# Attention in a two-layer step: full-height low-part score passes, and both heads' products with the values in alternation

## The chip, the cores and the metric

The kernel runs on one core of a Trainium2 chip. The metric is device time in microseconds for one execution. On the core, TensorE (PE in the profile) multiplies matrices, with its weight loads listed apart as PEld; VectorE (DVE), ScalarE (ACT) and GpSimd (POOL) do the elementwise work; SyncE (SP) issues nearly all DMA transfers. Each engine works through its own queue in order; the order of instructions in each queue is fixed when the kernel is built.

## The reference, cut to what matters

One inference step of a two-layer backbone over 128 prompt tokens and 256 sample tokens, width 1024. Layer 0 mixes tokens by attention, layer 1 by a gated MLP; each is followed by a gated feed-forward block. The change lies in layer 0's attention, 16 heads of 64 features:

```
# prompt: each head, 128 queries against 128 keys
s = einsum('bhqd,bhkd->bhqk', q, k) * HEAD_DIM ** -0.5
o = einsum('bhqk,bhkd->bhqd', softmax(s), v)

# sample: 256 queries on a grid of 4 rows x 64 columns; a window of all rows and 16 columns
# with a bias per head, and 128 cached context keys, in one softmax
s_win = einsum('bhqd,bhiqjd->bhqij', q_r, k_win) * scale + bias
s_ctx = einsum('bhqd,bhcd->bhqc', q_r, k_ctx) * scale
p = softmax(concatenate([s_win, s_ctx]))
o = einsum('bhqij,bhiqjd->bhqd', p_win, v_win) + einsum('bhqc,bhcd->bhqd', p_ctx, v_ctx)
```

All arithmetic is float32.

## The kernel before, in words

Features lie on partitions, the 384 tokens (prompt first) along the free axis. Every float32 operand of the large products is split exactly into a high and a low part (type fp32r): `load` brings a weight unit into `st` and writes `hi` (ACT) and `lo` (DVE); `mac` makes one product in three passes, high times high, high times low, low times high.

Attention goes over eight pairs of heads (`t`). For a pair, `keys(t)` takes 24 matmuls (8 feature tiles, three passes), copies the keys to `kT` beside the cached ones and splits them into `ks`, one tile per head: the high part on the 64 rows of the head, the low part on the other 64. `queries(t)` takes 24 matmuls and writes, per head, `qd` (the high part, twice over the 128 rows, by ACT) and its rows of `ql` (the low part, by DVE), one tile for both heads in two buffers. So `score` needs two passes: `qd` against all 128 rows of `ks`, then `ql` against the high part of the keys, which are the head's 64 rows only. `bias(t)` brings the position bias by four transfers into `btr` (one buffer) and adds the mask into `bt`.

`scores(t, hh)` makes a head's scores: two query blocks of the sample over 384 columns, one block of the prompt over 128, two passes each, so six matmuls, in two PSUM banks (`ps_sc`). DVE adds the bias and takes maxima, ACT does the exponential, DVE scales; the results are `pr` and `pc`. `values(t, ps)` turns the probabilities head by head: seven transposes (bank `ta`, then `tb`), two ACT copies into `pT`, and then that head's four products with the values, plain float32, each recorded as two matmul instructions of 64 columns. Head 0 takes columns 0 to 63 of the array, head 1 columns 64 to 127; results of both go to one bank `pv`, which is split into `ohi` and `olo` for the output projection.

Inside a pair the program order is scores of head 0, keys of the next pair, its bias, scores of head 1, queries of the next pair, values of the pair before, and then three units of the modulations (`ada.load(3)`, `ada.run(3)`: 24 instructions of 32 columns on the four column groups of the array). The framework takes program order as priority and moves an instruction up or down where operands are late by its own estimate, so that values and modulations stand among the first head's scores in PE's queue. The last pair's values come in the output projection, behind its second output tile.

The instructions in question: L462 and L463 are the two score passes, L524, L528 and L529 the transposes, L525 and L530 the copies to `pT`, L532 and L535 the products with the values, L190 the modulations, L103 to L105 the passes of `mac`.

Of the kernel before, what the change touches and what calls it, by code (L numbers as in the profile page):

```python
# [15 lines left out]
P = 128  # L16
D = 1024
KD = D // P                 # feature tiles of the model width
NPR = 128                   # prompt tokens
NSA = 256                   # sample tokens  # L20
NT = NPR + NSA              # all tokens, prompt first
GROUPS = ((0, 0, NPR), (1, NPR, NT))   # (conditioning, first token, end)
HD = 64
NPAIR = 8
E2 = 2048                   # gMLP width
# [7 lines left out]
# columns of the packed per-feature parameters  # L33
# [6 lines left out]
def backbone(ctx: ExitStack, tc: tile.TileContext, xT_in, cond_in, condr_in, b_ada_in, prm_in,  # L40
# [28 lines left out]
    nc.scalar.activation(zero, zero, AF.Silu)       # loads the table  # L69
# [7 lines left out]
    # TensorE runs at half its clock until it has been busy for a while  # L77
# [23 lines left out]
    def mac(out, a, b, start, stop):  # L101
        """out (+)= a.T @ b, both as (hi, lo)"""
        nc.tensor.matmul(out, a[0], b[0], start=start, stop=False)  # L103
        nc.tensor.matmul(out, a[0], b[1], start=False, stop=False)  # L104
        nc.tensor.matmul(out, a[1], b[0], start=False, stop=stop)  # L105
# [30 lines left out]
    def ada_block(f, tpool=ps_tb):  # L136
        """shift and scale of layer 0's mixer for feature tile f; TensorE's column groups take
        (half of the conditioning, shift or scale)"""
        pa = bank(ps_ad)
        w = ada_load(f) if f else w_first  # L140
        for kk in range(4):
            for hf in range(2):
                for q in range(2):
                    j = 2 * hf + q
                    nc.tensor.matmul(pa[32 * j:32 * j + 32, 0:P], cond_s[:, 4 * hf + kk, :],  # L145
                                     w[hf][:, kk, P * q:P * q + P], start=(kk == 0),
                                     stop=(kk == 3), tile_position=(0, 32 * j))
        sb = tmp.tile([P, 256], F32, name="ada_sb", tag="ada_sb")
        nc.scalar.copy(sb[:, :P], pa[:, :P])
        tp = bank(tpool)  # L150
        nc.tensor.transpose(tp[:, :P], sb[:, :P], ident)
        t = tp[:, :P].rearrange("p (h q r) -> p h q r", h=2, r=32)
        m = mods[0][:, 0:2, f]
        nc.vector.tensor_tensor(m, t[:, 0, :, 0:2],
                                b_ada[:, 0, 0:16].rearrange("p (q k) -> p q k", q=2)[:, :, f]
                                .unsqueeze(2).to_broadcast([P, 2, 2]), ALU.add)
        nc.vector.tensor_tensor(m, m, t[:, 1, :, 0:2], ALU.add)
        gain(0, CM, slice(f, f + 1))

    class Ada:  # L160
        """pieces of 1024 modulations on TensorE, one unit (a feature tile of the conditioning)
        at a time; units are loaded ahead of their products"""
# [35 lines left out]
        def flush(self):  # L198
            """[32j + conditioning, 256 columns] to features on partitions"""
# [18 lines left out]
    class AdaV:  # L218
        """modulations on VectorE, 128 at a time"""
# [40 lines left out]
    sq = {}  # L260

    def square(k, tag="t384"):
        """the last tile's squares are kept apart, to shorten what follows them"""
# [11 lines left out]
    def sums(pin=False):  # L275
        """every token's sum of squares"""
# [9 lines left out]
    def rms(ss=None, pin=False):  # L286
        """1/rms of every token, on all partitions: [P, NT] in PSUM"""
# [12 lines left out]
    def rsqrt(src, v, scale):  # L300
        """(src * scale + EPS) ** -0.5, refined by one Newton step"""
# [11 lines left out]
    # the modulated input of a layer's first products; its last two columns are the shifts  # L313
# [14 lines left out]
    # So that TensorE needn't wait for 1/rms, the first products of a layer take x * gain in place of  # L328
    # h and, in two more columns, the shifts; 1/rms and the shifts' products join them afterwards:
    # W.T @ h = (W.T @ (x * gain)) * R + W.T @ shift  # L330
# [9 lines left out]
    def norm_first(nxt, units):  # L340
        """the first tiles' products as the tiles of x come, then h; returns the banks and R"""
# [13 lines left out]
    def late(ps, R, wkp):  # L355
        """products with 1/rms, and the shifts' products to add to them"""
# [23 lines left out]
    def attention(pool, wkp):  # L380
        # 0 where key column cc is in the window of query column c, else NEG
# [15 lines left out]
        # V, all its tiles at once, as the tiles of h come  # L397
# [25 lines left out]
        # Scores are exact to float32 in two passes: the high part of q stands twice over the 128  # L423
        # rows, against the high and low parts of k; then its low part against the high part of k.
        # Head hh has its high part in rows hs.
# [18 lines left out]
        def queries(t):  # L444
# [5 lines left out]
            ql = wkp.tile([P, NT], F32R, name="ql", tag="ql", bufs=2)  # L450
            for hh in range(2):
# [3 lines left out]
                nc.vector.scalar_tensor_tensor(ql[a], pq[a, :NT], HD ** -0.5,  # L455
# [3 lines left out]
        def score(out, hh, q, ks, qs, cs):  # L459
            qd, ql = q  # L460
            a = HS[hh]
            nc.tensor.matmul(out, qd[hh][:, qs], ks[hh][:, cs], start=True, stop=False)  # L462
            nc.tensor.matmul(out, ql[a, qs], ks[hh][a, cs], start=False, stop=True)  # L463

        def bias(t):
            """relative position bias of query (row rr, column c) to key column cc, slot = key row -
            query row + 3 + rr; rpb_in has its columns reversed, so that both steps are positive"""
# [20 lines left out]
        def scores(t, hh, q, ks, bt):  # L488
            """softmaxes of a head: sample query blocks over window and cache, prompt"""
# [23 lines left out]
        def values(t, ps):  # L513
            """probabilities times values of both heads, as the pair's features"""
            pv = bank(ps_mm)
            for hh in range(2):
                pr, pc = ps[hh]
                hs = slice(64 * hh, 64 * hh + 64)
                pT = wkp.tile([P, 896], F32, name="pT", tag="pT", bufs=2)
                ta = bank(ps_ta)  # L520
                for kb in range(2):
                    for b in range(2):
                        o = kb * 256 + b * P
                        nc.tensor.transpose(ta[:, o:o + P], pr[:, b, kb * P:kb * P + P], ident)  # L524
                nc.scalar.copy(pT[:, 0:512], ta)  # L525
                tb = bank(ps_tb)
                for b in range(2):
                    nc.tensor.transpose(tb[:, b * P:b * P + P], pr[:, b, 256:384], ident)  # L528
                nc.tensor.transpose(tb[:, 256:384], pc, ident)  # L529
                nc.scalar.copy(pT[:, 512:896], tb[:, :384])  # L530
                vs = slice(P * t + 64 * hh, P * t + 64 * hh + 64)
                nc.tensor.matmul(pv[hs, 0:NPR], V[:, 0, vs], pT[:, 768:896], start=True, stop=True,  # L532
                                 tile_position=(0, 64 * hh))
                for i, vv in enumerate((V[:, 1, vs], V[:, 2, vs], cv[:, vs])):
                    nc.tensor.matmul(pv[hs, NPR:NT], vv, pT[:, 256 * i:256 * i + 256],  # L535
                                     start=(i == 0), stop=(i == 2), tile_position=(0, 64 * hh))
            split(ohi[t], olo[t], pv[:, :NT])

        # the values of a pair of heads come one pair after its scores
        kT, qT, bt = keys(0), queries(0), bias(0)  # L540
        old = None
        for t in range(NPAIR):
            new = [scores(t, 0, qT, kT, bt)]
            if t < NPAIR - 1:
                kT2 = keys(t + 1)
                bt2 = bias(t + 1)
            new.append(scores(t, 1, qT, kT, bt))
            if t < NPAIR - 1:
                qT, kT, bt = queries(t + 1), kT2, bt2
            if old is not None:  # L550
                values(t - 1, old)
# [5 lines left out]
        for m in range(KD):  # L557
# [7 lines left out]
            else:  # L565
                residual(0, GM, m, po, (0, SF, CF))
            if m == 1:
                values(NPAIR - 1, old)
# [6 lines left out]
    def conv(l, i, ps, wkp, tag):  # L575
        """ps: the tile's products, in PSUM or in SBUF"""
# [55 lines left out]
    def gmlp(pool, wkp):  # L632
        # a quarter of vn makes room for the low parts of four groups' results
# [95 lines left out]
def _layout(inp):  # L729
# [3 lines left out]
    def feat(a):        # (..., n*128) -> (128, ..., n)  # L733
# [13 lines left out]
    def units(w):       # (K, M) -> (M/128, 128 of K, K/128, 128 of M)  # L747
# [4 lines left out]
    # layer 0's first shifts and scales by feature tile and half of the conditioning  # L752
    w_ada0 = w_ada[0, :, :2 * D].reshape(2, 4, P, 2, KD, P).transpose(4, 0, 2, 1, 3, 5)
    # blocks of 128 modulations over all of the conditioning
# [43 lines left out]
```

## Time and profile before

| | |
|---|---|
| time, median of 3 runs | 1047.04 us (1046.14 to 1047.27) |
| profiled execution, span of the core | 1046.2 us |
| granted TensorE clock, mean | 0.990 |
| PE busy | 1027.7 us, 98% |
| DVE busy | 796.9 us, 76% |
| ACT busy | 496.8 us, 47% |
| mean DMA rate | 167 GB/s |

The page gives the span of the profiled execution, from the first to the last instruction, and no time of its own beside it; the median of the runs lies 0.8 us above that span. A busy time counts every instruction from its start to its end. Matmuls overlap in the array, so for PE the distance between two starts is the cost of the first of them. In the rows, `128*64` after the operands is the shape of the array that a matmul uses (rows, columns); behind it stand the partitions and columns of the data.

### The profile page before, as it was taken

How to read it: one execution, taken by the hardware profiler on the slowest of the kernel's cores; microseconds unless marked ns; L12 is line 12 of the kernel's file. 1: busy time of each engine (PE TensorE's matmuls, PEld its weight loads, DVE VectorE, ACT ScalarE, POOL GpSimd, SP SyncE). 2: the span in 40 equal slices, each digit the busy share in tenths (PEclk: the TensorE clock that was granted, in tenths of full speed). 3: DMA queues.
4: the chain of work that ended last, by engine and by line, in shares of the span. 5: the costliest groups of instructions: out<-in, count | busy, mean ns of one | idle time of the engine just before them, and what ended most of it. 6: DMA issues, size and time to landing. Idle time of an engine off the chain costs nothing.

```text
span 1046.2 us, 16013 instructions
## 1 busy us (share of the span) xinstructions
PE 1027.7 (98%) x5964; PEld 959.3 (92%) x5964; DVE 796.9 (76%) x1697; ACT 496.8 (47%) x862; POOL 13.3 (1%) x27
## 2 busy tenths in 40 slices
PE   7999999999999999999999999999999999999996
PEld 6787777679999999999998889999999999999995
DVE  3557666628899898999989979888599777777653
ACT  3357566536765544433346344444375544453330
POOL 1000000000000000000000000000000000000000
PEclk8999999999999999999999999999999999999998
DMA  7867666515255454566665765665414434435521
GB/s 274 310 191 208 187 186 194 192 61 171 81 153 181 161 156 150 161 199 211 217 196 174 247 205 157 198 191 195 144 65 157 142 122 123 134 109 169 163 69 61
DMA packets 64717, 174.32 MB, mean 167 GB/s; under 512 B 18800, under 2 KB 24064, under 8 KB 64640
## 3 DMA queue, kind: packets, MB, share of 16 engines
q1 hardware_dynamic: 63632, 171.46, 52.1%
q8 instruction: 47, 0.77, 0.3%
q0 software_dynamic: 432, 1.06, 0.3%
q10 hardware_dynamic: 576, 0.79, 0.2%
q14 instruction: 30, 0.25, 0.1%
HBM read 170.66 MB, written 2.62 MB: 166 GB/s over the span
## 4 chain that ended last, share of the span: by engine, by line
PE 92%; DMA 3%; DVE 2%; ACT 1%; SPq 1%; issue 1%; POOL 0%; POOLq 0%; DVEq 0%
PE bank L103 27%; PE bank L105 27%; PE bank L104 27%; DMA btr<-in_rpb 2%; PE bank L535 2%; PE bank L463 1%; PE bank L462 1%; PE bank L687 1%; PE bank L190 1%; PE bank L145 1%; PE bank L524 1%; DMA adw<-in_w_ada 1%; PE bank L532 1%; SPq L471 1%; PE bank L294 1%
## 5 line engine op out<-in xcount | busy, mean ns | idle before, releaser
L96 ACT CAST hi<-st 128x1024 fp32r<-128x1024 f32 (+1 forms) x216 | 222.5, 1032 | 315.3 <-PE bank L104 260.3
L105 PE MATMUL bank<-hhi,lo 128*128 128x384 f32 (+1 forms) x960 | 325.6, 339 | 0.4 <-DVE lo L97 0.4
L103 PE MATMUL bank<-hhi,hi 128*128 128x384 f32 (+1 forms) x960 | 325.7, 339 | 0.0
L104 PE MATMUL bank<-hlo,hi 128*128 128x384 f32 (+1 forms) x960 | 325.1, 339 | 0.0
L97 DVE TENSOR_TENSOR lo<-st,hi 128x1024 fp32r<-128x1024 f32 (+1 forms) x216 | 259.7, 1203 | 80.7 <-ACT hi L96 80.3
L103 PEld LDWEIGHTS bank<-hhi,hi 128*128 128x128 f32 x960 | 181.2, 189 | 3.5 <-issue 3.0
L105 PEld LDWEIGHTS bank<-hhi,lo 128*128 128x128 f32 x960 | 181.2, 189 | 1.3 <-DVE lo L97 0.7
L104 PEld LDWEIGHTS bank<-hlo,hi 128*128 128x128 f32 x960 | 180.6, 188 | 0.1
L248 DVE CUSTOM_DVE_ANT_0 junk<-adw,cs 128x1024 bf16<-128x1024 f32 x112 | 136.7, 1220 | 1.0
L105 PE MATMUL bank<-ahi,lo 128*128 128x384 f32 x352 | 119.0, 338 | 0.0
L104 PE MATMUL bank<-alo,hi 128*128 128x384 f32 x352 | 119.0, 338 | 0.0
L103 PE MATMUL bank<-ahi,hi 128*128 128x384 f32 x352 | 118.8, 338 | 0.0
L105 PEld LDWEIGHTS bank<-ahi,lo 128*128 128x128 f32 x352 | 66.1, 188 | 0.0
L104 PEld LDWEIGHTS bank<-alo,hi 128*128 128x128 f32 x352 | 66.1, 188 | 0.0
L103 PEld LDWEIGHTS bank<-ahi,hi 128*128 128x128 f32 x352 | 66.1, 188 | 0.0
L103 PE MATMUL bank<-hi,hhi 128*128 128x512 f32 x144 | 58.3, 409 | 1.8 <-ACT hhi L322 1.8
L105 PE MATMUL bank<-hi,hlo 128*128 128x512 f32 x144 | 57.5, 399 | 0.0
L104 PE MATMUL bank<-lo,hhi 128*128 128x512 f32 x144 | 57.4, 399 | 0.0
L368 DVE SCALAR_TENSOR_TENSOR x<-bank,mod,x 128x128 f32<-128x128 f32 x64 | 23.9, 413 | 37.6 <-PE bank L105 37.6
L103 PE MATMUL bank<-mhi,hi 128*128 128x384 f32 x128 | 43.4, 339 | 0.0
L105 PE MATMUL bank<-mhi,lo 128*128 128x384 f32 x128 | 43.2, 338 | 0.0
L104 PE MATMUL bank<-mlo,hi 128*128 128x384 f32 x128 | 43.1, 337 | 0.0
(151 smaller groups left out, 1288.7 us busy)
## 6 DMA issues: line engine op xcount, KB each, us to landing
st<-in_w_up SPq DMA_DIRECT2D x88, 512.0 KB, 3.5
adw<-in_w_adaT SPq DMA_DIRECT2D x56, 512.0 KB, 3.6
adw<-in_w_ada SPq DMA_DIRECT2D x40, 512.0 KB, 5.8
st<-in_w_down SPq DMA_DIRECT2D x32, 512.0 KB, 3.6
st<-in_w_qk SPq DMA_DIRECT2D x16, 512.0 KB, 6.7
st<-in_w_gu SPq DMA_DIRECT2D x16, 512.0 KB, 4.2
st<-in_w_gv SPq DMA_DIRECT2D x16, 512.0 KB, 4.3
st<-in_w_gout SPq DMA_DIRECT2D x16, 512.0 KB, 4.2
```

Source lines behind the costliest of these rows:

```text
L96: nc.scalar.copy(hi[:, :n], st[:, :n])
L97: nc.vector.tensor_tensor(lo[:, :n], st[:, :n], hi[:, :n].bitcast(F32), ALU.subtract)
L103: nc.tensor.matmul(out, a[0], b[0], start=start, stop=False)
L104: nc.tensor.matmul(out, a[0], b[1], start=False, stop=False)
L105: nc.tensor.matmul(out, a[1], b[0], start=False, stop=stop)
L145: nc.tensor.matmul(pa[32 * j:32 * j + 32, 0:P], cond_s[:, 4 * hf + kk, :], w[hf][:, kk, P * q:P * q + P], start=(kk == 0), stop=(kk == 3), ...
L190: nc.tensor.matmul(self.pa[32 * j:32 * j + 32, 0:256], cond_s[:, k, :], t[:, 256 * j:256 * j + 256], start=(k == 0), stop=(k == KD - 1), t ...
L248: tc.keep_in_program_order(nc.vector.tensor_tensor_reduce(self.junk, t, self.cs[c], 1.0, 0.0, ALU.mult, ALU.add, m[:, c:c + 1]))
L294: mm = nc.tensor.matmul(R[:, b * P:(b + 1) * P], r[:, b:b + 1].to_broadcast([P, P]), ident, start=True, stop=True)
L368: nc.vector.scalar_tensor_tensor(x[m][:, a:b], ps[:, a:b], mod(l, gate, m, c), x[m][:, a:b], ALU.mult, ALU.add)
L462: nc.tensor.matmul(out, qd[hh][:, qs], ks[hh][:, cs], start=True, stop=False)
L535: nc.tensor.matmul(pv[hs, NPR:NT], vv, pT[:, 256 * i:256 * i + 256], start=(i == 0), stop=(i == 2), tile_position=(0, 64 * hh))
```

## The change

Three things, and comments are dropped throughout.

1. `ql` becomes one tile per head, made once, 128 rows high. The half that doesn't belong to the head is set to zero once by POOL. DVE writes the head's half as before. The second score pass takes all 128 rows of `ql[hh]` against all 128 rows of `ks[hh]`; the zero rows meet the low part of the keys.
2. `values` is cut in two. `turned(hh, ps)` makes the seven transposes and two copies of one head, into `pT` with a tag per head and one buffer each. Head 0 of the pair before is turned after the scores of head 0, head 1 after the keys and the bias of the next pair. In the output projection the last pair is turned behind the first and the second output tile.
3. `values(t, pT)` then makes the products of both heads, head by head in turn for each operand, the sample's first and the prompt's last.

```
+        ql = [pool.tile([P, NT], F32R, name=f"ql{hh}") for hh in range(2)]
+        for hh in range(2):
+            nc.gpsimd.memset(ql[hh][64 * (1 - hh):64 * (1 - hh) + 64].bitcast(F32), 0.0)
...
-            ql = wkp.tile([P, NT], F32R, name="ql", tag="ql", bufs=2)
...
-                nc.vector.scalar_tensor_tensor(ql[a], pq[a, :NT], HD ** -0.5,
+                nc.vector.scalar_tensor_tensor(ql[hh][a], pq[a, :NT], HD ** -0.5,
                                                qd[hh][a].bitcast(F32), ALU.mult, ALU.subtract)
...
-            a = HS[hh]
             nc.tensor.matmul(out, qd[hh][:, qs], ks[hh][:, cs], start=True, stop=False)
-            nc.tensor.matmul(out, ql[a, qs], ks[hh][a, cs], start=False, stop=True)
+            nc.tensor.matmul(out, ql[hh][:, qs], ks[hh][:, cs], start=False, stop=True)
...
+        def turned(hh, ps):
+            pr, pc = ps[hh]
+            pT = wkp.tile([P, 896], F32, name="pT", tag=f"pT{hh}", bufs=1)
+            ta = bank(ps_ta)
+            for kb in range(2):
+                for b in range(2):
+                    o = kb * 256 + b * P
+                    nc.tensor.transpose(ta[:, o:o + P], pr[:, b, kb * P:kb * P + P], ident)
+            nc.scalar.copy(pT[:, 0:512], ta)
+            tb = bank(ps_tb)
+            for b in range(2):
+                nc.tensor.transpose(tb[:, b * P:b * P + P], pr[:, b, 256:384], ident)
+            nc.tensor.transpose(tb[:, 256:384], pc, ident)
+            nc.scalar.copy(pT[:, 512:896], tb[:, :384])
+            return pT
+
+        def values(t, pT):
             pv = bank(ps_mm)
+            def part(hh, cols, vv, o, n, start, stop):
+                nc.tensor.matmul(pv[64 * hh:64 * hh + 64, cols], vv[:, P * t + 64 * hh:P * t + 64 * hh + 64],
+                                 pT[hh][:, o:o + n], start=start, stop=stop, tile_position=(0, 64 * hh))
+
+            for i, vv in enumerate((V[:, 1], V[:, 2], cv)):
+                for hh in range(2):
+                    part(hh, slice(NPR, NT), vv, 256 * i, 256, i == 0, i == 2)
             for hh in range(2):
...
+                part(hh, slice(0, NPR), V[:, 0], 768, 128, True, True)
             split(ohi[t], olo[t], pv[:, :NT])
...
             new = [scores(t, 0, qT, kT, bt)]
+            if old is not None:
+                pT = [turned(0, old)]
             if t < NPAIR - 1:
                 kT2 = keys(t + 1)
                 bt2 = bias(t + 1)
+            if old is not None:
+                pT.append(turned(1, old))
             new.append(scores(t, 1, qT, kT, bt))
             if t < NPAIR - 1:
                 qT, kT, bt = queries(t + 1), kT2, bt2
             if old is not None:
-                values(t - 1, old)
+                values(t - 1, pT)
...
+            if m == 0:
+                pT = [turned(0, old)]
             if m == 1:
-                values(NPAIR - 1, old)
+                pT.append(turned(1, old))
+                values(NPAIR - 1, pT)
```

More of the change, by code (lines that the diff above doesn't have):

```diff
@@ L511, in scores @@
             return pr, pc
-        def values(t, ps):
-            pv = bank(ps_mm)
-            for hh in range(2):
[L517 to L536, printed above, removed]
@@ L541, in attention @@
         old = None
+        pT = None
         for t in range(NPAIR):
             new = [scores(t, 0, qT, kT, bt)]
+            if old is not None:
+                pT = [turned(0, old)]
             if t < NPAIR - 1:
```

## The prediction

> **What bounds the kernel now.** I read the line of the engines on the page first. TensorE (PE) is busy throughout, so a change of PE work can move the end.
>
> ```profile
> span 1046.2 us, 16013 instructions
> PE 1027.7 (98%) x5964; PEld 959.3 (92%) x5964; DVE 796.9 (76%) x1697; ACT 496.8 (47%) x862; POOL 13.3 (1%) x27
> ```
>
> Next, the windows view over four successive head pairs of the attention loop (cut from one uninterrupted score block to the next), and the waits of PE between 72 and 240 us, where the whole loop lies.
>
> ```profile
> 113.65:133.52 19.87, 19.75 (x117) 14.75 (x117) 13.13 (x40) 12.54 (x28) 0.54 (x1) 1.00 0.59 175
> 133.52:152.90 19.38, 19.38 (x117) 14.68 (x117) 12.79 (x39) 11.10 (x26) 0.54 (x1) 1.00 0.63 175
> 152.90:172.40 19.50, 19.50 (x113) 14.48 (x113) 13.35 (x39) 12.27 (x27) 0.54 (x1) 1.00 0.68 200
> 172.40:192.20 19.80, 19.80 (x117) 14.74 (x117) 13.63 (x49) 13.07 (x36) 0.54 (x1) 1.00 0.63 222
> ```
>
> ```profile
> PE bank L463 <- DVE ql L455: 0.5, 1, 0.5
> PE bank L105 <- DVE lo L97: 0.4, 1, 0.4
> PE bank L524 <- ACT pT L525: 0.3, 1, 0.3
> ```
>
> Columns of the windows: stretch, length, then busy time of PE, weight loads, VectorE (DVE), ScalarE (ACT) and POOL, the granted clock, the DMA share, GB/s. A pair takes 19.6 us on average and PE is busy for all of it; DVE has 13.2 us, ACT 12.2. PE waited 1.2 us in all. So the loop's length is the sum of PE's start-to-start times, and a busy figure says little, because matmuls overlap: starts have to be read. The timeline of PE shows them (start, duration, line).
>
> ```profile
> 113.29 0.34 PE L104 MATMUL bank<-hlo,hi 128*128 128x384 f32 x1
> 113.47 0.34 PE L105 MATMUL bank<-hhi,lo 128*128 128x384 f32 x1
> 113.65 0.34 PE L462 MATMUL bank<-ks,qd 128*128 128x384 f32 x1
> 113.91 0.44 PE L463 MATMUL bank<-ks,ql 64*128 64x384 f32 x1
> 114.28 0.33 PE L462 MATMUL bank<-ks,qd 128*128 128x128 f32 x1
> 114.54 0.32 PE L463 MATMUL bank<-ks,ql 64*128 64x128 f32 x1
> 114.79 0.44 PE L462 MATMUL bank<-ks,qd 128*128 128x384 f32 x1
> 115.16 0.44 PE L463 MATMUL bank<-ks,ql 64*128 64x384 f32 x1
> 115.53 0.44 PE L103 MATMUL bank<-hhi,hi 128*128 128x384 f32 x1
> 115.81 0.34 PE L104 MATMUL bank<-hlo,hi 128*128 128x384 f32 x1
> ...
> 119.67 0.34 PE L105 MATMUL bank<-hhi,lo 128*128 128x384 f32 x1
> ```
>
> Plain 384-column products start 0.175 us apart: 22 steps from 115.81 to 119.67. But each step between a 128-row and a 64-row pass lengthens both sides: the same 384 columns take 0.37 us among the alternating passes, and the first product after the block takes 0.28. The array's shape changes six times here and each change costs. That is the first thing the edit touches. The second is in this stretch, one visit of the values (L532, L535) for one head, and the modulations' products (L190):
>
> ```profile
> 101.05 0.27 PE L529 MATMUL bank<-ident,pc 128*128 128x128 f32 x1
> 101.25 1.50 PE L190 MATMUL bank<-adw,cond_s 128*32 128x256 f32 x24
> 102.68 0.44 PE L462 MATMUL bank<-ks,qd 128*128 128x384 f32 x1
> ...
> 104.39 0.55 PE L524 MATMUL bank<-ident,pr 128*128 128x128 f32 x3
> 104.87 0.43 PE L532 MATMUL bank<-pT,V 128*64 128x128 f32 x2
> 105.14 1.03 PE L535 MATMUL bank<-pT,V 128*64 128x256 f32 x4
> 106.00 0.59 PE L535 MATMUL bank<-pT,cv 128*64 128x256 f32 x2
> 106.53 0.33 PE L524 MATMUL bank<-ident,pr 128*128 128x128 f32 x1
> 106.70 0.38 PE L528 MATMUL bank<-ident,pr 128*128 128x128 f32 x2
> ```
>
> An instruction of the values with 256 columns comes every (106.00 - 105.14) / 4 = 0.215 us: all stand in the same half, one after another. The 24 of L190, also 256 columns, take 1.43 us until the next start, 0.06 each: they go round four column groups, and four run side by side (0.215 / 0.06 is 3.6, the change of shape behind them included).
>
> **The change, part by part.**
>
> *Low-part passes over 128 rows.* The count of instructions stays; the 64-row shape goes. The block above lasts from 113.65 to 115.81 less one plain product, 2.16 - 0.175 = 1.985 us. In one shape it is four passes of 384 columns at 0.175 and two of 128 columns, for which the nearest rows are the transposes of 128 columns in the same shape (two of L528 take 0.38 us where one, as L529, takes 0.27, so they start 0.11 apart): 0.92 us. Gain 1.065 us, 0.178 for each of the six changes. How many there are:
>
> ```profile
> L463 PE MATMUL bank<-ks,ql x48: 322/436/442, 75.8 to 212.9; 64*128 64x384 f32 x32, 64*128 64x128 f32 x16
> L535 PE MATMUL bank<-pT,V x64: 378/379/380, 105.1 to 231.0; 128*64 128x256 f32 x64
> ```
>
> The 48 low passes (16 blocks) would have 96 changes; walking PE's timeline from the first to the last of them I count 84 that vanish, since some passes stand next to each other or next to column-split work, where a change remains. 84 x 0.178 = 14.9 us. Bounds: a 128-column pass may cost down to 128/384 of 0.175 (0.06) or as much as the slowest 128-column row here (0.26, from 114.28 to 114.54). 32 of them make that 1.6 us more or 4.8 less. I take 0.11, a measured pace in the same shape.
>
> *Both heads' products alternate.* Before: a visit runs from 104.87 to 106.53, 1.66 us, plus what the change of shape adds to the transpose ahead (the third of L524 starts at 104.39 + 0.55 - 0.27 = 104.67, so 0.20 against 0.11: 0.09) and to the one behind (0.17 from 106.53 to 106.70: 0.06): 1.81 us. The 64 of L535 on V are four to a visit: 16 visits. After: one visit for both heads, 6 rounds at 0.216 and 2 at 0.11 as two halves run together, 1.51 us, and 0.30 for the changes: 1.81, eight times. Gain 8 x 1.81 = 14.5 us. Bounds: with no overlap of the halves only one pair of changes goes, 8 x 0.30 = 2.4 us; with full overlap 14.5. I take full overlap, nearest to L190's rows, whose groups write one bank as these do.
>
> The Trainium skill (TensorE: Matmul & The Clock Gate, "Measured speedup vs the span model") has three column tiles at 2.38 times, 79% of three. By that the halves would reach 1.59 and the eight visits would cost about 3 us more than my sum, an estimate from that page. The L190 rows lie closer to full, so they decide.
>
> *Turning early.* The 14 transposes and four ACT copies of a pair stay; they move to behind the first head's scores and behind the keys' products. Neither queue gains an instruction, no DMA moves past SP. What they used to cover is the gap between the queries' products and the next scores, where ACT writes qd and DVE ql. What is left there is the values (1.8 us) and the modulations (1.43 us), 3.2 us, against a chain of three operations:
>
> ```profile
> L454 ACT ACTIVATE qd<-bank 64x384 fp32r<-64x384 f32 x16 | 7.8, 485 | 0.2
> L455 DVE SCALAR_TENSOR_TENSOR ql<-bank,qd 64x384 fp32r<-64x384 f32 x16 | 8.8, 553 | 7.8 <-ACT qd L454 7.7
> L485 DVE RECIPROCAL st<-st 128x1 f32<-128x1 f32 x48 | 7.4, 158 | 6.6 <-ACT pr L484 6.3
> ```
>
> Two qd at 0.485 and one ql at 0.553 are 1.5 us, so the cover holds unless ACT is a full 1.7 us late; were it gone, up to 1.5 us per pair, 12 us over the loop. The probabilities to be turned are a pair old, so the transposes find them.
>
> *ql held once, two POOL memsets.* The tiles take the place of two buffers of the same size. DVE writes ql after the queries' products, which stand behind the last low pass in PE's order (block at 113.65, products from 115.53): nothing. The memsets run on POOL, busy for 13.3 us of the span, before ql is first needed at 75.8: nothing.
>
> *What does not arrive.* The chain of waits leaves PE before 95 us:
>
> ```profile
> 80.50 8.77 DMA btr<-in_rpb
> 90.42 0.96 DVE bt L477
> 93.36 1.15 DVE lo L97
> 94.55 0.44 PE bank L105
> ```
>
> Until 94.55 the bias table's transfer and DVE set the pace, and PE waited for DVE there. Of the 84 changes, 14 lie ahead of that: 14 x 0.178 = 2.5 us, of which I count 2 as lost. Later, with 29.4 / 8 = 3.7 us gone from a pair of 19.6, PE needs 15.9 and DVE's 13.2 plus its waits for ACT in this loop ((7.7 + 6.3) / 8 = 1.75) make 15.0. The margin is 0.9 us on average and will be overrun in some pairs: 0 to 8 us, I take 3.
>
> **Sum.** -14.9 - 14.5 + 2 + 3 = -24.4 us. Against the profiled span of 1046.2 that is 1021.8; the median of the three runs is 1047.0, 0.8 above it, so 1022.6 in those terms.
>
> **Rivals.**
>
> *DVE and ACT become the bound.* For it: 15.0 against 15.9 us. Against: in the windows DVE's busy time counts accumulator reads that overlap the operation before them. At 1 us of PE waits in each pair beyond my 3: 1030. The Trainium skill (TensorEngine Tiling (Array Packing), "PSUM Bottleneck") warns of this: packing speeds up TensorE, not the emptying of PSUM. The trace bears it out only so far, ACT's 12.2 us a pair being well under 15.9.
>
> *The halves don't overlap.* For it: no two-half stream exists in this trace. Against: L190. Then 1047.0 - 14.9 - 2.4 + 2 = 1032 (the slack stays, no stalls).
>
> *The low pass gains nothing,* its long start-to-start time belonging to the pass and not to the change of shape. Against it: L462, already 128 rows, is as slow among them (0.37) and 0.18 behind a plain product would be its own pace. Then 1047.0 - 14.5 + 1 = 1034.
>
> *Slower: ql in one buffer.* If the queries' products were ordered ahead of the second head's scores, DVE's write of ql for the next pair would stand in DVE's queue until those scores had been taken, and the softmaxes queued behind it would wait, which hold the score banks. One block of 24 products (24 x 0.175 = 4.2 us) per pair would be added against 3.7 gained: 8 x 0.5 = 4 us, 1051. It decides from 3.7 us a pair on. Against it: the order now has the scores first, and nothing pulls the queries forward.
>
> **How the numbers follow.** Forecast as summed, 1016 to 1027: 0.70. DVE/ACT bound, around 1030: 0.13. No overlap: 0.07. No gain from the low pass: 0.05. Slower: 0.03. No visible effect: 0.02. The range goes from 1015 (1047.0 - 29.4 - 1.6, less a us) to 1033, which takes in the two nearest rivals. A change of 0.2% (2 us) is about what can be told from no change here. Faster 0.95, same 0.02, slower 0.03.
>
> **What would show it.** Score blocks between products lasting about 0.9 us, with all six passes as 128*128; the values' instructions starting in pairs a few ns apart, two per 0.216 us, in eight visits of about 1.5 us; pairs of about 16 us in the windows; the times behind the loop unchanged. It is wrong if PE shows waits of more than some 5 us between 72 and 232 us, if the halves start 0.2 us apart, or if the 128-column passes still take 0.25.

## The result, and the profile after

The changed kernel takes 1030.8 us (median of 4 runs, 1029.4 to 1035.4) against 1047.15 us before: a ratio of 0.9847, 95% interval 0.9832 to 0.9863, or 16.3 us gained. The profiled execution has a span of 1028.7 us, 17.5 below the one before. The forecast was 1022, between 1015 and 1033: the direction and the range hold, the number is 9 us too low.

The page of the changed kernel, engine line and two strips:

```profile
span 1028.7 us, 16012 instructions
PE 1001.3 (97%) x5964; PEld 953.1 (93%) x5964; DVE 796.0 (77%) x1697; ACT 496.2 (48%) x862; POOL 14.1 (1%) x29
PE   7999897999999999999999999999999999999996
PEclk8999898999999999999999999999999999999998
```

PE lost 26 us of busy time and the other engines nothing, but PE is no longer busy throughout: the slices from 103 to 129 and from 154 to 180 us have an 8 and a 7, and the granted clock falls to 8 tenths in both. Both are inside the attention loop. The windows view, cut as before from score block to score block, and PE's waits between 72 and 240 us:

```profile
93.80:109.30 15.50, 15.32 (x114) 13.48 (x115) 13.03 (x42) 12.09 (x29) 0.54 (x1) 1.00 0.75 216
109.30:130.80 21.50, 18.89 (x118) 15.60 (x117) 13.49 (x40) 12.60 (x28) 0.54 (x1) 0.84 0.67 178
130.80:146.00 15.20, 15.20 (x118) 13.50 (x116) 11.92 (x38) 11.16 (x28) 0.54 (x1) 1.00 0.68 192
146.00:162.10 16.10, 15.59 (x116) 13.36 (x114) 12.12 (x35) 11.39 (x25) 0.54 (x1) 1.00 0.62 189
162.10:184.90 22.80, 18.11 (x118) 14.66 (x117) 14.54 (x53) 13.97 (x39) 0.54 (x1) 0.85 0.71 256
```

```profile
PE bank L464 <- ACT qd L457: 6.9, 4, 4.7
PE bank L464 <- ACT pc L486: 1.8, 1, 1.8
PE bank L206 <- ACT ada_sb L195: 0.8, 1, 0.8
PE bank L465 <- DVE ql L458: 0.2, 1, 0.2
PE bank L464 <- ACT pr L486: 0.2, 1, 0.2
```

Three pairs take 15.2 to 16.1 us, where the forecast for an average pair was 15.9. The other two take 21.5 and 22.8 us, longer than any pair before the change, and in them the clock is 0.84 and 0.85. PE's waits add up to 9.9 us, against 1.2 before. PE's timeline shows the two edits themselves (L464 and L465 are now the score passes, L538 the products with the values):

```profile
109.31 0.42 PE L464 MATMUL bank<-ks,qd 128*128 128x384 f32 x1
109.56 0.33 PE L465 MATMUL bank<-ks,ql 128*128 128x384 f32 x1
109.73 0.22 PE L464 MATMUL bank<-ks,qd 128*128 128x128 f32 x1
109.79 0.27 PE L465 MATMUL bank<-ks,ql 128*128 128x128 f32 x1
109.90 0.39 PE L464 MATMUL bank<-ks,qd 128*128 128x384 f32 x1
110.13 0.34 PE L465 MATMUL bank<-ks,ql 128*128 128x384 f32 x1
110.31 0.34 PE L103 MATMUL bank<-hhi,hi 128*128 128x384 f32 x1
...
114.61 1.08 PE L538 MATMUL bank<-pT,V 128*64 128x256 f32 x8
115.52 0.60 PE L538 MATMUL bank<-pT,cv 128*64 128x256 f32 x4
115.95 0.39 PE L538 MATMUL bank<-pT,V 128*64 128x128 f32 x4
116.27 1.07 PE L190 MATMUL bank<-adw,cond_s 128*32 128x256 f32 x16
119.00 0.44 PE L464 MATMUL bank<-ks,qd 128*128 128x384 f32 x1 [1.65 <-ACT qd L457]
```

The score block lasts 1.00 us, from 109.31 to 110.31, against 1.985. The values of both heads last 1.66 us (114.61 to 116.27), for which two visits took twice that before: four instructions of 256 columns on cv start within 0.43 us, 0.11 each. And in the last line PE stands 1.65 us for qd, behind its cover.

### The profile page after: what moved, and what is told of

It reads as the page before. It is cut to its first block, busy times and chain, and to the rows that moved or that the text cites. A ratio compares the mean times of both kernels' runs of the same rounds, so it can differ in the third digit from the quotient of the medians.

```text
span 1028.7 us, 16012 instructions
## 1 busy us (share of the span) xinstructions
PE 1001.3 (97%) x5964; PEld 953.1 (93%) x5964; DVE 796.0 (77%) x1697; ACT 496.2 (48%) x862; POOL 14.1 (1%) x29
## 4 chain that ended last, share of the span: by engine, by line
PE 88%; DMA 4%; DVE 3%; issue 2%; ACT 2%; POOL 0%; SPq 0%; POOLq 0%; DVEq 0%; ACTq 0%
PE bank L103 28%; PE bank L104 27%; PE bank L105 27%; DMA st<-in_w_qk 1%; PE bank L704 1%; PE bank L145 1%; DMA st<-in_w_o 1%; DMA btr<-in_rpb 1%; PE bank L190 1%; PE bank L538 1%; DMA out_skT<-kT 1%; PE bank L280 1%; PE bank L294 0%; ACT hi L96 0%; DMA cond<-in_cond 0%
## 5 line engine op out<-in xcount | busy, mean ns | idle before, releaser
L96 ACT CAST hi<-st 128x1024 fp32r<-128x1024 f32 (+1 forms) x216 | 222.6, 1033 | 325.8 <-PE bank L104 261.6
```

The costliest lines, as they stand in the source:

```text
L96: nc.scalar.copy(hi[:, :n], st[:, :n])
```

## Where the time went

Two chains of rows explain the long pairs. The first, ACT and DVE between 111 and 119 us (the part in brackets is the idle time ahead and what ended it):

```profile
111.11 1.05 ACT L96 CAST hi<-st 128x1024 fp32r<-128x1024 f32 x1 [1.81 <-DMA st<-in_w_qk]
112.19 1.22 DVE L97 TENSOR_TENSOR lo<-st,hi 128x1024 fp32r<-128x1024 f32 x1 [3.88 <-ACT hi L96]
113.45 1.40 DVE L445 TENSOR_TENSOR ks<-kT,ks 64x512 fp32r<-64x512 f32 x2
114.88 0.43 DVE L502 CUSTOM_DVE_ANT_0 bank<-bank,bt 128x256 f32<-128x256 f32 x1
116.26 0.58 ACT L486 ACTIVATE pr<-bank,st 128x384 f32<-128x384 f32 x1 [1.94 <-DVE st L507]
118.46 0.48 ACT L457 ACTIVATE qd<-bank 64x384 fp32r<-64x384 f32 x1
```

The scores of 109.31 are first looked at by DVE at 114.88, 5.6 us later. Ahead of that step in DVE's queue stand the subtraction for a weight unit, which waited for ACT's cast, which waited for the unit's transfer, and the split of the next pair's keys. None of it is urgent: that unit's products start at 123.5. The exponentials are late by as much, and qd stands behind them in ACT's queue. The second chain is shorter:

```profile
170.01 1.04 ACT L96 CAST hi<-st 128x1024 fp32r<-128x1024 f32 x1 [4.95 <-DMA st<-in_w_o]
...
174.40 1.01 PE L464 MATMUL bank<-ks,qd 128*128 128x384 f32 x2 [4.66 <-ACT qd L457]
```

ACT stood 4.95 us for the first unit of the output projection, with the exponentials and qd of the pair behind it. With each of the two comes a stretch at half clock, here behind the first:

```profile
125.25 0.52 PE L103 MATMUL bank<-hhi,hi 128*128 128x384 f32 x1
125.57 0.52 PE L104 MATMUL bank<-hlo,hi 128*128 128x384 f32 x1
125.89 0.52 PE L105 MATMUL bank<-hhi,lo 128*128 128x384 f32 x1
```

Products that start 0.175 us apart at full clock are 0.32 apart. In windows of half a us and one us the granted clock is 0.50 from 121.1 to 127.9 us and from 172.3 to 179.1, 6.8 us each. PE stood in waits for 0.8 us of the first stretch and 2.1 us of the second, so the lower clock itself cost (6.8 - 0.8) / 2 = 3.0 us in the one pair and (6.8 - 2.1) / 2 = 2.4 in the other. With 8.7 us more of waits that is 14.1 us lost, where the forecast had 5 (2 in the first pairs, 3 of waits). Taken back from the 17.5 us of the spans, PE's sequence itself is shorter by 31.6 us; the sum had 29.4.

So one theory, called A below: PE's sequence shrank as summed, and what is missing was lost to transfers that land after the place which ACT's queue holds for their cast. B: ACT and DVE work is the bound. Later C: the order of work on DVE and ACT.

## Experiments

**The low-part pass alone** (`e1_low_only`: the kernel before with item 1 of the change).

> The kernel before with the full-height low-part pass alone (one ql tile per head, zeros in the other half); values as before. Theory A (the change shortens PE's sequence by 14.9 us here and 14.5 us by the alternation, and what is missing of the sum went into PE waits behind late weight transfers and the half clock after them): the pairs shrink from 19.6 us by about 1.9, ACT and DVE keep slack, so few waits: 1032 to 1035 us. Theory B (ACT and DVE work is the bound at some 16.5 us a pair): the same, since 17.7 us is above it. If the long pass were the price of the pass itself and not of the change of shape: 1046.

Measured: 1040.5 us, ratio 0.9935 (0.9911 to 0.9959), a gain of 6.9 us. The expectation missed. The block is what it should be:

```profile
113.19 0.34 PE L464 MATMUL bank<-ks,qd 128*128 128x384 f32 x1
...
114.11 0.34 PE L103 MATMUL bank<-hhi,hi 128*128 128x384 f32 x1
```

0.92 us from first pass to first product, the forecast to the digit. That settles the rival by which the long passes were slow of themselves. But PE's waits between 72 and 240 us rose from 1.2 to 6.2 us, on pT (2.7 in all), on casts and subtractions of weight units, and on qd: already 1.9 us less per pair is more than the transfers and queues follow. The 8.2 us by which the profiled span is shorter (1038.0 us) and these 5.0 us of waits make 13.2 of the 14.9 of the sum.

**The 64-row pass put back** (`e2_low_64`: the change without item 1).

```
+            ql = wkp.tile([P, NT], F32R, name="ql", tag="ql", bufs=2)
...
-            nc.tensor.matmul(out, ql[hh][:, qs], ks[hh][:, cs], start=False, stop=True)
+            nc.tensor.matmul(out, ql[a, qs], ks[hh][a, cs], start=False, stop=True)
```

> The changed kernel with the low-part pass put back on 64 rows (ql for both heads in one tile, two buffers); early turning and alternation stay. Theory A: pairs of 17.7 us, about 14.5 us gained over the kernel before less 2 in the first pairs, and few PE waits: 1032 to 1036 us. Theory B: the same. If the halves overlapped less than the rows suggest: above 1038.

Measured: 1035.8 us, ratio 0.9887 (0.986 to 0.9914), a gain of 11.6 us, inside what both theories gave. Item 1 alone gives 6.9 us, items 2 and 3 without it 11.6; together they give 16.3, a little less than the sum of the two.

**Products head by head** (`e3_no_turns`).

```
-            for i, vv in enumerate((V[:, 1], V[:, 2], cv)):
-                for hh in range(2):
-                    part(hh, slice(NPR, NT), vv, 256 * i, 256, i == 0, i == 2)
             for hh in range(2):
+                for i, vv in enumerate((V[:, 1], V[:, 2], cv)):
+                    part(hh, slice(NPR, NT), vv, 256 * i, 256, i == 0, i == 2)
                 part(hh, slice(0, NPR), V[:, 0], 768, 128, True, True)
```

> The changed kernel with the products head by head (all of head 0, then all of head 1) in one visit: the overlap is undone, 8 x 1.5 = 12 us come back on PE. Theory A: PE's pairs grow to 16.6 us, which gives the late transfers time, so a part of the 10 us of waits goes: 1034 to 1040 us against 1030.8. Theory B: PE was not the bound in the changed kernel, so at most 3 us are lost: 1031 to 1034.

Measured: 1032.8 us, ratio 0.9861 (0.984 to 0.9883); the interval overlaps that of the change, so the 2.0 us are not resolved. The time lies in B's range (1031 to 1034) and below A's (1034 to 1040), but it can't decide between them, for the edit did not do what its expectation says. PE's timeline within such a visit, in which all eight instructions of head 0 (four on V, two on cv, two of 128 columns on V) stand ahead of head 1's in PE's queue:

```profile
114.67 1.08 PE L538 MATMUL bank<-pT,V 128*64 128x256 f32 x4
115.59 0.38 PE L538 MATMUL bank<-pT,cv 128*64 128x256 f32 x1
115.59 0.43 PE L538 MATMUL bank<-pT,V 128*64 128x256 f32 x1
115.81 0.38 PE L538 MATMUL bank<-pT,cv 128*64 128x256 f32 x1
115.86 0.81 PE L538 MATMUL bank<-pT,V 128*64 128x256 f32 x5
```

A second product on V starts at 115.59 beside the first on cv, which can only be head 1's, ahead of head 0's second on cv (115.81). So the halves overlap without alternation too, from the fifth instruction on, and a visit takes 2.58 us (114.67 to 117.25) instead of 1.66: some 7 us over eight, not 12. PE's waits fell by 3.2 us (from 9.9 to 6.7) and the half clock by half.

**Turning late** (`e4_turn_late`: both heads turned just ahead of their products, `values(t - 1, [turned(0, old), turned(1, old)])`).

> The changed kernel with both heads turned just ahead of their products, as before, 14 transposes in one place; low pass and alternation stay. Theory A: PE's sequence is as long as in the changed kernel, the waits stay or move, because they hang on the transfers: 1027 to 1034 us. If the early turning took away the cover between the queries' products and the next scores, and this is what costs: 1022 to 1026.

Measured: 1031.8 us, ratio 0.9855 (0.9833 to 0.9876), no different from the change. PE's waits are 7.8 us there, 4.3 of them for pT: they moved, as A has it. The transposes' place is not what costs.

**The transfer that SP stands for** (`f1_kt_kept`). SP works in order, and the load of the cached keys into kT waited for the store of older keys out of the same buffer. Two kept tiles make it wait only for the readers of its own columns:

```
+        kTs = [pool.tile([P, 512], F32, name=f"kT{i}") for i in range(2)]
-            kT = wkp.tile([P, 512], F32, name="kT", tag="kT", bufs=2)
+            kT = kTs[t % 2]
```

> The changed kernel with kT as two tiles kept for the whole loop and used in turn, so that the transfer of the cached keys into columns 384 to 511 waits only for the splits that read those columns and no longer for the transfer that stores the prompt's keys; SP stood 39 us at that wait, with the weight units queued behind it. Theory A (PE waits come from weight units that land after the place where ACT's queue holds their cast): units are asked for up to 9 us earlier, 1020 to 1027 us. Theory B (ACT and DVE work is the bound): no change, 1029 to 1033. A third, the transfers being slow for bandwidth and not late for their issue: no change either, and f4 tells.

Measured: 1025.2 us, ratio 0.9792 (0.9777 to 0.9806), 5.6 us below the change. SP's wait at this place, in the change and then with kept tiles, between 60 and 240 and between 60 and 200 us:

```profile
SPq L434 <- DMA out_skT<-kT: 39.4, 5, 9.9
```

```profile
SPq L436 <- DVE ks L447: 19.6, 4, 8.7
```

The wait for the store is gone, PE's waits are 5.0 us instead of 9.9, and one half-clock stretch is left instead of two. SP is no freer, though: it still stands 19.6 us at this place, now for the split, and 48.0 us instead of 29.1 (60 to 200 us) until the low part of an older weight unit is made. What did fall are ACT's waits for weight units between 72 and 210 us, in the change and then with kept tiles (the kernel before had 3.1 us of them):

```profile
ACT hi L96 <- DMA st<-in_w_qk: 7.5, 6, 2.2
ACT hi L96 <- DMA st<-in_w_o: 5.0, 1, 5.0
```

```profile
ACT hi L96 <- DMA st<-in_w_qk: 3.1, 3, 2.4
ACT hi L96 <- DMA st<-in_w_o: 1.1, 1, 1.1
```

A's number came out; what it says of the rest, next.

**Casts pinned behind older work** (`f2_pins`, and with kept tiles `f3_pins_kt`): units asked for one stage ahead in the program, their cast and subtraction kept behind what precedes them.

```
-            nc.scalar.copy(hi[:, :n], st[:, :n])
+            a1 = nc.scalar.copy(hi[:, :n], st[:, :n])
...
+            if pin:
+                tc.keep_in_program_order(a1)
+                tc.keep_in_program_order(a2)
```

> The changed kernel with each weight unit of the loop asked for one stage ahead and its cast and its subtraction kept behind what precedes them in the program on ACT and DVE, so that a cast cannot stand ahead of older exponentials. Theory A: the softmaxes are no longer held by a transfer; PE waits below 3 us in the loop, no half clock, 1018 to 1026 us. Theory B: 1029 to 1033. Against the edit itself: if the casts now come too late, PE waits at the first product of a block, up to 2 us in each of 14 blocks.

> Both edits (kept kT tiles, pinned casts one stage ahead). Theory A: the better of the two alone or up to 3 us below it, 1017 to 1024 us. Theory B: 1029 to 1033.

Measured: 1030.2 us (0.984, 0.9825 to 0.9855) and 1027.0 us (0.9813, 0.9798 to 0.9828). Pinning alone gains nothing over the change, and on top of the kept tiles nothing over 1025.2. A missed in both (1018 to 1026, 1017 to 1024), and B's range held in the first. Half clock went from the loop in the first, and ACT's waits for weight units with it (12.5 us in the change between 72 and 210 us, none here), but PE still waited 6.6 us. So taking the late units out of ACT's way does not by itself bring the time down: A in the form "the cast stands too early" gets no support here.

**Less to transfer** (`f4_no_mod_loads`: 20 of the 24 units of TensorE's modulations are not brought in; the first four are used over again).

```
+                if len(self.kept) < ADA_BUFS:
                     t = adp.tile([P, D], F32, name="adw", tag="adw")
...
+                else:
+                    t = self.kept[k % ADA_BUFS]
```

> The changed kernel with only the first four of the 24 units of the modulations brought in by TensorE's part in attention, these being used over and over: 10 MB of transfers are left out, the products stay. Theory A: the weight units land sooner (median below 5 us against 7.9), the waits of ACT for them go, 1018 to 1024 us. Theory B: 1028 to 1032, since no work of ACT, DVE or PE is taken away.

Measured: 1029.1 us (0.9834, 0.9817 to 0.985), and the weight units' median time from issue to landing was 8.7 us, not below 5. A's numbers missed, B's range held. SP still stood 26.7 us for the key store. So it is not the amount of data that makes units late. In f1 that median is 7.9 us, as in the change, so f1 did not shorten the transfers either; what it can have changed is when units are asked for.

**Kept tiles in the kernel before** (`g4_before_kt`: the edit of f1 on the old kernel).

> The kernel before with kept kT tiles and nothing else. Theory A: its pairs of 19.6 us left the transfers time, PE waited 1.2 us in all, so the edit that gave 5.6 us in the changed kernel gives at most 1 us here: 1045.7 to 1047.7. If the wait at the key store delays every kernel of this kind alike: 1041 to 1043.

Measured: 1046.6 us, ratio 0.9989 (0.998 to 0.9999), 0.6 us. The wait was in the old kernel too, 31 us of it on SP, and cost nearly nothing while pairs took 19.6 us.

**The bias one pair ahead** (`g1_bias_ahead`, with kept tiles: `bias(t + 2)` behind the queries' products).

> The changed kernel with kept kT tiles, and the bias of a pair asked for and masked one pair earlier, behind the queries' products, so that DVE's mask step no longer stands among the second head's softmaxes waiting for its transfer (0.94 us once at 113 us in the run with kept kT). Theory A (PE waits come from transfers that hold ACT's and DVE's queues): another 1 to 4 us below the 1025.2 of kept kT alone, 1021 to 1025 us. If what is left is the order of work on DVE and not the transfer: 1025 to 1028.

Measured: 1026.5 us, ratio 0.9797 (0.9767 to 0.9828), no better than kept tiles alone.

**Head by head with kept tiles** (`g2_kt_no_turns`).

> The changed kernel with kept kT tiles and the products head by head, so the overlap is undone (8 x 1.5 = 12 us of PE's sequence). In the changed kernel the same step cost 2.0 us (1032.8 against 1030.8). Theory A: with fewer waits more of the 12 us shows, 5 us or more: 1030 to 1035 us against 1025.2. If the loop is bound by something other than PE whatever the transfers do: 1026 to 1028.

Measured: 1026.1 us, ratio 0.9798 (0.9768 to 0.9827), not to be told from 1025.2. The visits take 2.6 us here too. So some 7 us on PE's path did not show, with fewer waits around: in this kernel PE's sequence was not yet what set the end. That speaks against A as it stood, and for something in the chain from scores to qd.

**The keys' split behind the second head's scores** (`h1_split_late`, with kept tiles). In f1 the first maximum of the second head's scores of 107.9 us began at 112.18, behind a weight unit's subtraction and the split of the next keys, which nobody needs before the next pair.

```
+            return kT
+
+        def key_parts(kT):
             ks = [wkp.tile([P, 512], F32R, name="ks", tag=f"ks{hh}", bufs=2) for hh in range(2)]
...
             new.append(scores(t, 1, qT, kT, bt))
             if t < NPAIR - 1:
+                kT2 = key_parts(kT2)
```

> The changed kernel with kept kT tiles, and the split of the next pair's keys (two casts on ACT, two subtractions on DVE, 1.4 us there) traced behind the second head's scores and no longer ahead of them, so that the second head's maxima and exponentials don't queue behind it. Theory C (after kept kT, what is left hangs on the order of work on DVE and ACT between the second head's scores and qd, in the pair from 108 to 129 us above all: the first maximum began 4.3 us after the scores): the exponentials end 1.5 to 3 us earlier, PE's wait for qd and the half clock behind it go, 1018 to 1023 us. Theory A alone (late transfers hold the queues, whatever the order): 1024 to 1027, as with kept kT.

Measured: 1021.8 us (5 runs, 1018.0 to 1023.5), ratio 0.9753 (0.9733 to 0.9773), the fastest version here. The same DVE step in f1 and in h1, each with the scores at 107.9 and 107.7 us:

```profile
112.18 0.43 DVE L504 CUSTOM_DVE_ANT_0 bank<-bank,bt 128x256 f32<-128x256 f32 x1
```

```profile
110.21 0.42 DVE L507 CUSTOM_DVE_ANT_0 bank<-bank,bt 128x256 f32<-128x256 f32 x1
```

The pair in question in both, and PE's waits of h1:

```profile
107.90:128.90 21.00, 18.99 (x120) 15.54 (x118) 13.55 (x40) 12.56 (x28) 0.54 (x1) 0.84 0.74 211
```

```profile
107.70:124.90 17.20, 15.84 (x120) 13.60 (x117) 13.21 (x40) 12.61 (x29) 0.54 (x1) 1.00 0.75 200
124.90:140.00 15.10, 15.10 (x117) 13.41 (x115) 11.75 (x38) 11.11 (x27) 0.54 (x1) 1.00 0.77 211
140.00:155.80 15.80, 15.40 (x117) 13.40 (x115) 12.96 (x39) 11.95 (x27) 0.54 (x1) 1.00 0.83 248
155.80:173.00 17.20, 15.90 (x118) 13.49 (x116) 13.60 (x49) 13.00 (x36) 0.54 (x1) 1.00 0.77 276
```

```profile
PE bank L206 <- ACT ada_sb L195: 2.1, 2, 1.4
PE bank L469 <- ACT qd L462: 0.7, 2, 0.5
PE bank L470 <- DVE ql L463: 0.4, 1, 0.4
```

The maximum comes 2.0 us earlier, the waits for qd fall from 3.2 us (f1) to 0.7, no clock below 1.00 is left in these pairs, and the pair of 21.0 us takes 17.2. ACT and DVE do nearly the same work as in f1 (ACT 12.6 us in that pair in both, DVE 13.2 against 13.6), so B as a bound by work is out: the order was it. C is what the run shows, on top of f1's edit. The gain over f1 is 3.4 us; the profile is that of the fastest of the five runs, 3.8 us below their median.

## Why the prediction was right or wrong

The range held because it was drawn out to 1033 to take in the two nearest rivals. The forecast as summed, 1016 to 1027 with a chance of 0.70, missed, and a sign that the prediction had named for being wrong came: PE's waits are 9.9 us, above its 5. Some of it is luck, too: PE's sequence shrank by about 2 us more than summed, which hid a part of what waits and half clock took.

*The bound and the two prices: right.* Pairs without a long wait are at 15.2 to 16.1 us. The price of a change of shape (0.178 us) is borne out by e1's block of 0.92 us, that of the overlap by the visit of 1.66 us (1.81 forecast, 0.15 of it in the steps at both ends, which the 1.66 leaves out). In h1, where 3.2 us of waits and no half clock are left in the loop, the profiled span is 1016.2: 30.0 us below before, close to the 29.4 of the sum without its deductions. A round of the two halves takes 0.215 us (115.52 to 115.95 holds two), as one instruction did, so the overlap of two is full in this trace. By the 79% from the Trainium skill (TensorE: Matmul & The Clock Gate, "Measured speedup vs the span model") the visits would have taken 3 us more in all, an estimate from that page that this trace doesn't bear out.

*The term of waits: mis-sized.* "0 to 8, I take 3" was read from averages, DVE's busy time plus its waits on ACT per pair against PE's. What came was not spread: two waits of some microseconds, in two of the pairs, and with each a half clock that the sum had no term for. With the waits of the first pairs these make 14.1 us where 5 stood. The margin of 0.9 us on average says nothing of a queue in which a subtraction that waits for a transfer stands ahead of a maximum.

*"Neither queue gains an instruction, no DMA moves past SP": true and not enough.* Nothing was added, but with 4 us gone from a pair every transfer has 4 us less from its issue to the place of its cast, and SP's wait for the key store, free before (g4), was worth 5.6 us after (f1). The prediction named a cover of 3.2 us and the point at which it fails, ACT 1.7 us late; it did not ask what could make ACT late. That is the step that failed.

*Early turning: right*, as far as the noise lets it be told, that it costs nothing (e4). *Alternation:* the gain comes from one visit for both heads as much as from the order inside it, since the halves overlap in part in any order (e3).

*The rivals.* "DVE and ACT become the bound" gave 1030 and so the measured time, and the chain runs through them; but not as it was put, since neither is short of time. The warning of the Trainium skill (TensorEngine Tiling (Array Packing), "PSUM Bottleneck") pointed the right way: PE did end up waiting for what ACT reads out of PSUM, 6.9 us for qd. The remedy was not faster emptying but emptying in time. The rivals without overlap and without gain in the low pass are refuted by the rows above, and the one that ends slower, ql in one buffer, did not occur: the scores kept their place ahead of the queries' products (110.13 and 110.31), and PE's waits for ql are 0.2 us.

*Left open:* the sequence shrank by some 32 us in the profiles of the change and of h1 (31.6, and 30.0 with 2.0 more of waits than before), 2 to 3 more than summed. In the change 0.7 us of that stands ahead of anything changed: the first score block starts at 73.12 us, against 73.83. The score blocks don't give the rest. Their high-part pass of 128 columns takes 0.06 us (109.73 to 109.79) instead of 0.11, but the pass two behind it takes 0.23 (109.90 to 110.13) instead of 0.175. The rest is not accounted for. How much of f1's gain is the issue on SP and how much the new order that came with it was not separated.

## What to carry to other kernels

When an edit shortens an engine that is busy all the time, look up for each queue beside it what stands ahead of the step that this engine needs next, and how late the transfers behind that may be; averages of busy time don't show it. Work that nobody needs for a while belongs behind the urgent chain in the program; for the split of the next keys that was worth 3.4 us here, while pinning the casts of prefetched weights gained nothing. A prefetch shouldn't stand in one queue with a load that waits for a store (5.6 us here). Mixed shapes of the array have a price at each change, here 0.18 us, so a half-filled pass padded with zeros can be cheaper than the smaller shape.

## What the runs showed of the hardware

Matmuls on the second column half start ahead of earlier queued ones on the first half, once those stand in line: in e3, head 1's first at 115.59 while three of head 0's were still to start (one on cv at 115.81, two of 128 columns). The Trainium skill (TensorE: Matmul & The Clock Gate, "The mechanism") has matmuls in strict program order in their starts; these rows differ from that.

Half clock followed short idle times. In the changed kernel's first long pair the longest recorded wait of PE is 1.65 us (until 119.00), and about 2 us later the clock is halved for a stretch. In the second it is halved at 172.3 us, 2.6 us into a wait of 4.66 (169.74 to 174.40). The Trainium skill (TensorE: Matmul & The Clock Gate, "What's actually happening") speaks of an idle window of about 3.4 us; both drops came with less idle time than that. No run here has separated the sum of several short waits from one long one.
